# Block 1's late LayerNorms: sums placed behind the early products, and no modulation dots emitted in the product parts ahead of them

## The chip, the cores and the metric

The kernel runs on one NeuronCore of one Trainium2 chip. Five engines work side by side, each through its own list of instructions in a fixed order: TensorE (PE), VectorE (DVE), ScalarE (ACT), GpSimd (POOL) and SyncE (SP), which issues all loads. The metric is the time of one execution on the device in microseconds (us); less is better.

## The reference, cut to what matters

Two transformer blocks on 256 tokens of width 1024, in fp32. The first has two layers. In each, a vector `c` gives six modulation vectors (`silu(c) @ w_ada[l] + b_ada[l]`), and both LayerNorms sum over the width of the whole updated stream, so nothing behind a norm is complete before the last quarter of the product ahead of it.

```python
def layer_norm(x, g, b):
    mu = xf.mean(-1, keepdims=True)
    var = jnp.square(xf - mu).mean(-1, keepdims=True)
    return (xf - mu) * lax.rsqrt(var + LN_EPS) * g + b

def first_block(...):
    for l in range(DEPTH):                                   # 2 layers
        sh1, sc1, g1, sh2, sc2, g2 = split(silu(c) @ w_ada[l] + b_ada[l], 6)
        y = mixer(x * (1 + sc1) + sh1) @ w_o[l]
        x = layer_norm(ALPHA * x + (1 + g1) * y, ln_g[l, 0], ln_b[l, 0])
        y = swiglu(x * (1 + sc2) + sh2, w_ffn_in[l], w_ffn_out[l])
        x = layer_norm(ALPHA * x + (1 + g2) * y, ln_g[l, 1], ln_b[l, 1])
    return x

def swiglu_half_step(x, g, mod, j, w_up, w_down):            # second_block
    h = rms_norm(x, g) * (1 + mod[j + 1]) + mod[j]
    gt, up = split(h @ w_up, 2)
    return x + 0.5 * mod[j + 2] * ((silu(gt) * up) @ w_down)
```

The second block has two layers too. Each begins with such a half step on the stream `x` (the first block's result) and on a context stream `c` that the first block doesn't touch. Its nine modulation vectors exist once for each stream (from `c` and `c_ctx`) and come from the same matrix `w_ada_2[l]`.

## The kernel before, in words

**Products.** Activations lie with the width on the 128 partitions (8 tiles of 128 by 256 tokens). An fp32 product is three fp32r products: weights and activations are split into a high and a low part (`wh`, `wl` and `hh`, `hl`, line 149), and PE multiplies wh by hh, wl by hh, and wh by hl (line 131). So 128 output features of one stream cost 24 matmuls over a width of 1024. A weight unit is loaded to `raw` (up to 512 KB, three buffers), cast to `wh` on ACT and subtracted to `wl` on DVE (six buffers of each). A pair of units gives a PSUM bank `ps_mm` of which there are two. All loads go through SP's one queue in program order: a load whose buffer isn't free holds up those behind it.

**Modulation dots.** No matmul is used for the modulation vectors. Tile `adaw` (512 KB, two buffers) holds 128 rows of the modulation matrix, and one DVE instruction (line 456, output `junk`) multiplies it by the broadcast vector `cb` and sums along it. In block 1 a load serves one dot, in block 2 two (one for each stream). A generator `self.ada` makes load and dots in a fixed order of vectors, eight loads for each vector.

**The order.** The program is written out by a planner. Generators ("threads") for `x`, for `c`, and for the norms make the instructions piece by piece, and `main` picks the next piece by a clock of its own. `pace`, called between pieces, earns credit for dots by a rate for each phase and emits them; while `self.calm` is set it earns none. When the `x` thread needs a modulation vector that isn't complete, `until` emits all that is left of it at that place, one load and its dots after another. The `c` thread can't do that: it stays parked until the vector is there, and the planner goes on with others. `meet` merges a product of `x` and one of `c` on the same weights into a joint one (512 columns) when both have come to it.

**Late LayerNorms.** Three of block 1's four LayerNorms (layer 0's two, layer 1's first; below the first, second and third) are late. While the product ahead (attention's `w_o`, or the FFN's down product) comes out in four pairs of tiles, `emit` adds each pair to `x_res` (line 756, `add_gated`), makes the un-normalised operand with `late_tile` (lines 532 and 533), and adds squares and values up in two tiles `acc` (line 494). Only then `early` (lines 278 to 325) multiplies three pairs of units by the un-normalised operand in all six PSUM banks of `ps_mm`, `ps_s` and `ps_o`: 36 matmuls over the first six tiles, 12 over the last two, then 24 for each further unit (144 in all). `ln_finish` (from line 572), a thread of the highest priority, sums over the partitions by matmuls with `ones` (`ps_t`: four of `acc`, then four of `x_res` and four of `tr`, each of these over two tiles), reduces (line 587), goes through a chain of small DVE instructions (lines 348 to 359, 594), spreads the two columns by matmuls with `c_ident` (line 136), and updates `x_res` (line 610). With what that leaves, line 477 makes the normalised operand and `post` (lines 296 to 300) corrects and frees the early banks. `early` sets `calm` at its beginning and clears it at its end. The fourth LayerNorm, at the end of block 1, isn't late: behind it stand the RMS norm of `x` (`rms`: sums, line 634, chain, spread, and lines 650 to 653, which need the modulation vectors 1 and 0) and the first products of block 2. The `c` thread is started in layer 1's FFN and works on its own RMS norm and its first products there.

Of the kernel before, what the change touches and what calls it, by code (L numbers as in the profile page):

```python
# [67 lines left out]
class Block:  # L68
# [503 lines left out]
    def ln_finish(self, key, x, g, b, late=None):  # L572

        nc = self.nc
        st = self.p("t", (128, 2, 2, 2))
        (ax, lx), (aq, lq) = self.acc.pop((key, 0)), self.acc.pop((key, 1))
        sl = [slice(0, 128), slice(128, 256)]
# [84 lines left out]
    def ffn(self, h, wi, wo, emit, gate, last_gate=None):  # L662
# [4 lines left out]
        late = isinstance(h, Late)  # L667
        hf = None if late else self.ops(h)
        per = 12
        for i0 in range(0, FT, per):  # L670
# [26 lines left out]
            left = -(-(FT - i0 - ni) // per)  # L697
            yield ("need", gate if left or last_gate is None else last_gate)
            parts = [(i0 + k, min(6, ni - k)) for k in range(0, ni, 6)]
            for mp in range(4):  # L700
                blocks = (2 * mp, 2 * mp + 1)
                if late and mp < 2 and len(parts) == 1:

                    units = tuple(wo + (b,) + parts[0] for b in blocks)
                    yield ("w", units)
                    two = [self.p(tag, (128, 256)) for tag in ("mm", "s")]
                    for ks in ((0, -1), (-1, None)):
                        for u, ps in zip(units, two):
                            self.feat(ps, self.weight(u), 0, gf, 0, True, True, *ks)
                else:  # L710
                    ps = yield from self.feats(wo, blocks, gf, parts)
                    two = [ps[:, j, :] for j in range(2)]
                emit(left, mp, two)

    def ffn_pair(self, th, wi, wo, emit, gate):

# [420 lines left out]
    def block1(self, x, cx, ct):  # L1137
        nc = self.nc
        for l in range(2):
# [40 lines left out]
            yield ("need", ("a1", l, 3))  # L1180
            gb = self.ln_g[:, l, 0, :], self.ln_b[:, l, 0, :]
            h = self.ln_late(*gb, P(3), P(4))
            yield from self.half_out(("w_o", l), box["o"], 4, emit)
            self.spawn(self.ln_finish("b", x, *gb, h), -1)
            self.phase = ("f", l)
# [668 lines left out]
```

## Time and profile before

| | |
|---|---|
| runs, median | 2626.09 us |
| runs, lowest and highest (3) | 2618.99 and 2626.55 us |
| profiled execution, its own time | 2625.82 us |
| profiled execution, span of the trace | 2624.0 us |
| granted TensorE clock, mean of the span | 0.967 of full |
| PE, DVE, ACT, POOL busy | 95%, 66%, 40%, 8% |
| mean DMA rate | 156 GB/s |

The span is what the trace shows from first to last instruction; the profiled execution's own time is 1.8 us longer. All times below in rows are microseconds from the span's start. Busy PE time contains overlapping records, so two matmuls' distance is read from their starts.

### The profile page before, as it was taken

Reading aid. Unit: us, or ns where it says so; the run is one execution under the profiler, and the core shown is the slowest. Engines: PE = TensorE matmul, PEld = TensorE weight load, DVE = VectorE, ACT = ScalarE, POOL = GpSimd, SP = SyncE. Lnnn points to the kernel's source line nnn. Section 1 sums busy time; section 2 is a strip of 40 time slices with the busy share of each in tenths; the row PEclk is TensorE's granted clock in tenths of the full one; section 3 lists DMA queues with packets and bytes.
Section 4 is the critical chain, followed back from the end, with each engine's and each line's share of the span. In section 5 each row is a group of like instructions: output and inputs, shape, how many; then the busy total and the mean of one; then the engine's idle time right before and its main releaser. Section 6 shows DMA issues by size and latency. Waiting matters only on the chain.

```text
span 2624.0 us, 40217 instructions
## 1 busy us (share of the span) xinstructions
PE 2491.1 (95%) x15668; PEld 2239.9 (85%) x15668; DVE 1743.6 (66%) x3255; ACT 1046.2 (40%) x1817; POOL 220.9 (8%) x243
## 2 busy tenths in 40 slices
PE   5989998999998999999989999999999999999999
PEld 4879998989997888889788888888888888988999
DVE  6788887588887765576666757465754445576754
ACT  3555444545443222233566322222322223365543
POOL 2111003121000000000252000000000000041000
PEclk9989998889998999999989899999999999989999
DMA  7776885546763644534311245454354443431564
GB/s 280 248 235 210 287 283 188 180 147 194 232 189 115 192 145 133 155 113 137 106 32 49 85 154 171 118 171 127 114 167 146 128 129 105 129 96 42 174 192 133
DMA packets 127071, 408.92 MB, mean 156 GB/s; under 512 B 15585, under 2 KB 21281, under 8 KB 126753
## 3 DMA queue, kind: packets, MB, share of 16 engines
q1 hardware_dynamic: 126880, 406.35, 49.4%
q8 instruction: 123, 2.02, 0.3%
q14 instruction: 68, 0.55, 0.1%
HBM read 405.22 MB, written 1.07 MB: 155 GB/s over the span
## 4 chain that ended last, share of the span: by engine, by line
PE 75%; DVE 11%; DMA 6%; ACT 4%; issue 3%; POOL 1%; SPq 0%; ACTq 0%; DVEq 0%; POOLq 0%
PE ps_mm L131 65%; PE ps_o L131 3%; PE ps_s L131 3%; DMA raw<-in_w_ffn_in 3%; DVE wl L149 3%; PE ps_t L136 2%; PE ps_t L131 2%; DVE junk L456 2%; ACT wh L149 1%; DMA raw<-in_w_ffn_out 1%; DVE hmem L653 1%; DVE tr L650 1%; DMA adaw<-in_w_ada 1%; POOL tr L475 1%; ACT e L785 1%
## 5 line engine op out<-in xcount | busy, mean ns | idle before, releaser
L131 PE MATMUL ps_mm<-hmem,wh 128*128 128x256 f32 (+1 forms) x5760 | 1386.3, 331 | 49.8 <-ACT hmem L473 21.6
L131 PEld LDWEIGHTS ps_mm<-hmem,wh 128*128 128x128 f32 x5760 | 997.0, 195 | 159.3 <-ACT hmem L473 22.0
L131 PE MATMUL ps_mm<-hmem,wl 128*128 128x256 f32 (+2 forms) x2880 | 950.9, 330 | 2.1 <-DVE wl L149 2.0
L149 ACT CAST wh<-raw 128x1024 fp32r<-128x1024 f32 (+2 forms) x572 | 546.0, 958 | 867.8 <-PE ps_mm L131 371.7
L149 DVE TENSOR_TENSOR wl<-raw,wh 128x1024 fp32r<-128x1024 f32 (+2 forms) x556 | 625.5, 1128 | 355.6 <-ACT wh L149 353.4
L131 PEld LDWEIGHTS ps_mm<-hmem,wl 128*128 128x128 f32 x2880 | 558.9, 194 | 49.9 <-DVE wl L149 2.9
L131 PE MATMUL ps_mm<-g,wh 128*128 128x256 f32 (+1 forms) x2328 | 534.1, 323 | 3.8 <-ACT g L149 3.8
L456 DVE SCALAR_TENSOR_TENSOR junk<-adaw,cb 128x1024 fp8e4<-128x1024 f32 x343 | 423.1, 1233 | 27.8 <-DMA adaw<-in_w_ada 23.3
L131 PEld LDWEIGHTS ps_mm<-g,wh 128*128 128x128 f32 x2328 | 393.0, 191 | 37.5 <-ACT g L149 4.0
L131 PE MATMUL ps_mm<-g,wl 128*128 128x256 f32 (+1 forms) x1164 | 375.3, 322 | 2.5 <-DVE wl L149 2.5
L131 PEld LDWEIGHTS ps_mm<-g,wl 128*128 128x128 f32 x1164 | 222.9, 191 | 19.3 <-DVE wl L149 2.9
L965 POOL TENSOR_TENSOR kk<-kT,kk 64x512 fp32r<-64x512 f32 (+1 forms) x30 | 35.7, 1189 | 1359.6 <-ACT kk L964 1358.5
L735 DVE TENSOR_TENSOR tr<-tr,ps_mm 128x512 f32<-128x512 f32 x61 | 42.0, 688 | 144.9 <-PE ps_mm L131 144.9
L734 ACT ACTIVATE tr<-ps_mm 128x512 f32<-128x512 f32 x61 | 36.5, 598 | 242.6 <-PE ps_mm L131 242.6
L756 DVE SCALAR_TENSOR_TENSOR x_res<-ps_mm,ada_x,x_res 128x256 f32<-128x256 f32 x144 | 67.0, 481 | 92.0 <-PE ps_mm L131 91.5
L131 PEld LDWEIGHTS ps_o<-g,pt 128*128 128x128 f32 x808 | 109.4, 207 | 11.2 <-ACT pt L371 7.4
L131 PE MATMUL ps_o<-g,pt 128*128 128x64 f32 (+1 forms) x808 | 111.8, 287 | 4.8 <-ACT pt L371 4.5
L785 ACT ACTIVATE e<-e,small 128x256 f32<-128x256 f32 (+2 forms) x160 | 90.7, 568 | 34.9 <-DVE small L779 33.8
L131 PE MATMUL ps_mm<-wh,hmem 128*128 128x256 f32 x512 | 94.1, 282 | 0.0
L136 PE MATMUL ps_t<-c_ident,e 128*128 128x128 f32 x404 | 69.8, 297 | 12.9 <-ACT e L785 5.8
L131 PEld LDWEIGHTS ps_mm<-wh,hmem 128*128 128x128 f32 x512 | 79.5, 188 | 0.6 <-ACT g L371 0.6
L149 ACT CAST g<-tr 128x256 fp32r<-128x256 f32 (+1 forms) x137 | 68.3, 499 | 25.2 <-DVE tr L681 10.9
(227 smaller groups left out, 2034.5 us busy)
## 6 DMA issues: line engine op xcount, KB each, us to landing
adaw<-in_w_ada SPq DMA_DIRECT2D x231, 512.0 KB, 4.4
raw<-in_w_ffn_up SPq DMA_DIRECT2D x176, 512.0 KB, 3.9
raw<-in_w_ffn_in SPq DMA_DIRECT2D x88, 512.0 KB, 4.6
raw<-in_w_ffn_down SPq DMA_DIRECT2D x96, 384.0 KB, 3.1
raw<-in_w_ffn_out SPq DMA_DIRECT2D x48, 384.0 KB, 4.0
raw<-in_w_in SPq DMA_DIRECT2D x28, 512.0 KB, 3.7
raw<-in_w_in_ab SPq DMA_DIRECT2D x16, 512.0 KB, 6.6
raw<-in_w_o SPq DMA_DIRECT2D x16, 512.0 KB, 4.8
```

The costliest lines, as they stand in the source:

```text
L131: self.tc.keep_in_program_order(self.nc.tensor.matmul(out, left, right, start=start, stop=stop))
L136: self.tc.keep_in_program_order(self.nc.tensor.transpose(out, in_, self.ident))
L149: return (self.nc.scalar.copy(hi, src), (eng or self.nc.vector).tensor_tensor(out=lo, in0=src, in1=hi.bitcast(F32), op=OP.subtract))
L456: ins = self.nc.vector.scalar_tensor_tensor(out=self.junk, in0=raw, scalar=1.0, in1=v, op0=OP.mult, op1=OP.mult, accum_out=acc[:, j:j + 1] ...
L475: nc.gpsimd.tensor_scalar(out=h32[:, j, :], in0=src[:, j, :], scalar1=a[:, k0 + j:k0 + j + 1], scalar2=b[:, k0 + j:k0 + j + 1], op0=OP.mul ...
L650: nc.vector.scalar_tensor_tensor(out=t[:, j, :], in0=x[:, k + j, :], scalar=a[:, k + j:k + j + 1], in1=bc, op0=OP.mult, op1=OP.mult)
L653: nc.vector.scalar_tensor_tensor(out=hl[:, k + j, :T], in0=t[:, j, :], scalar=b[:, k + j:k + j + 1], in1=hh[:, k + j, :T].bitcast(F32), op ...
L734: nc.scalar.activation(sg, job.full[0], AF.Silu)
L735: nc.vector.tensor_tensor(out=sg, in0=sg, in1=job.full[1], op=OP.mult)
L756: self.nc.vector.scalar_tensor_tensor(out=x[:, k, :], in0=ps[j], scalar=gate[:, k:k + 1], in1=x[:, k, :], op0=OP.mult, op1=OP.add)
L785: nc.scalar.activation(e[:, at:at + w], e[:, at:at + w], AF.Exp, bias=nm, scale=-1.0, accum_out=sm)
L965: self.nc.gpsimd.tensor_tensor(out=there, in0=k, in1=here.bitcast(F32), op=OP.subtract)
```

## The change

Three edits. First, `ln_finish` with a late operand waits 2.5 units of the planner's clock before its first sums, so that other pieces are written out ahead of them. Second, `ffn` sets `calm` for the second to fourth pair of the last part of its down product, and clears it at the end. Third, block 1 sets `calm` ahead of the second half of the `w_o` product (it stays set until `early` clears it).

```diff
@@ def ln_finish(self, key, x, g, b, late=None):
         nc = self.nc
+        if late is not None:
+
+            yield self.after(2.5)
         st = self.p("t", (128, 2, 2, 2))
@@ def ffn(self, h, wi, wo, emit, gate, last_gate=None):
             for mp in range(4):
                 blocks = (2 * mp, 2 * mp + 1)
+                self.calm = left == 0 and mp > 0
                 if late and mp < 2 and len(parts) == 1:
...
                 emit(left, mp, two)
+        self.calm = False
@@ block 1, each layer
             h = self.ln_late(*gb, P(3), P(4))
+            self.calm = True
             yield from self.half_out(("w_o", l), box["o"], 4, emit)
             self.spawn(self.ln_finish("b", x, *gb, h), -1)
```

Numbers in names below are the program's running numbers and differ between the two programs; lines from 575 on stand 3 to 6 further down in the changed one.

On PE at the first late LayerNorm, the end of the `w_o` product (`ps_mm` of 256 columns), the four sums of `acc` and the first early products (258 columns). Before:

```order
L131 MATMUL ps_mm_1736<-hmem,wh_1739 128x256
L131 MATMUL ps_t_1781<-ones,acc_1642 128x1
L131 MATMUL ps_t_1781<-ones,acc_1640 128x1
L131 MATMUL ps_t_1781<-ones,acc_1642 128x1
L131 MATMUL ps_t_1781<-ones,acc_1640 128x1
```

and in the changed program, where the last early matmul over the sixth tile stands ahead of the sums and the first over the seventh tile behind them:

```order
L131 MATMUL ps_mm_1770<-hmem,wh_1783 128x258
L131 MATMUL ps_t_1823<-ones,acc_1642 128x1
L131 MATMUL ps_t_1823<-ones,acc_1640 128x1
L131 MATMUL ps_t_1823<-ones,acc_1642 128x1
L131 MATMUL ps_t_1823<-ones,acc_1640 128x1
L131 MATMUL ps_mm_1769<-hmem,wh_1777 128x258
```

The four sums moved behind the 36 early matmuls over six tiles. The sums of `x_res` and `tr`, which stood behind those 36, now stand behind all of the first pair and the next unit (72), and between them and the spread 48 matmuls stand instead of 36. It is so at all three late LayerNorms.

On PE at the end of block 1. Before: the fourth LayerNorm's sums (`ps_t<-ones`), products of `c` on `w_ffn_up` (`ps_mm<-hmem`), the LayerNorm's spread (`c_ident,small`), products of `c`, the RMS sums of `x` (the second `ones,acc`), their spread, and the first product of `x`.

```order
L131 MATMUL ps_t_8569<-ones,x_res 128x1 x4
L131 MATMUL ps_t_8569<-ones,tr_8567 128x1 x4
L131 MATMUL ps_mm_8574<-hmem,wh_8639 128x256
...
L136 MATMUL ps_t_8705<-c_ident,small_8623 128x128 x2
L136 MATMUL ps_t_8705<-c_ident,small_8635 128x128 x2
L131 MATMUL ps_mm_8674<-hmem,wh_8742 128x256
...
L131 MATMUL ps_t_8777<-ones,acc_8716 128x1
...
L136 MATMUL ps_t_8799<-c_ident,small_8787 128x128 x2
L131 MATMUL ps_mm_8834<-hmem,wh_8577 128x256
```

In the changed program, with the RMS sums of `c` (`acc_7383`) behind those of `x`:

```order
L131 MATMUL ps_t_8480<-ones,x_res 128x1 x4
L131 MATMUL ps_t_8480<-ones,tr_8478 128x1 x4
L136 MATMUL ps_t_8517<-c_ident,small_8499 128x128 x2
L136 MATMUL ps_t_8517<-c_ident,small_8511 128x128 x2
L131 MATMUL ps_t_8576<-ones,acc_8528 128x1
...
L131 MATMUL ps_t_8598<-ones,acc_7383 128x1
...
L136 MATMUL ps_t_8620<-c_ident,small_8586 128x128 x2
L131 MATMUL ps_mm_8651<-hmem,wh_8654 128x256
```

Before, the steps of `x` had 24, 48 and 24 matmuls of `c` between them, and `c`'s own RMS norm stood within the last down product. In the changed program no product stands between the last down product and the first one of `x`; behind that come 24 matmuls of `x`, the spread of `c`, 24 of `x` and 48 of `c`, and then 144 joint ones, where before 96 of `x` and 96 joint ones stood.

On DVE at the same place, the end of LayerNorm's update (now line 613), the last sums of squares (`acc`) and the chain of `x`'s RMS norm. Before (first rows), and in the changed program (rows behind the dots):

```order
L494 TENSOR_TENSOR acc_8716<-acc_8716,tr_8722 128x256
L610 TENSOR_TENSOR x_res<-x_res,ps_t_8705 128x512
L494 TENSOR_TENSOR acc_8716<-acc_8716,tr_8722 128x256
L494 TENSOR_TENSOR acc_8716<-acc_8716,tr_8730 128x256 x2
L634 TENSOR_SCALAR small_8784<-ps_t_8777 128x2
```

```order
L494 TENSOR_TENSOR acc_8528<-acc_8528,tr_8534 128x256
L456 SCALAR_TENSOR_TENSOR junk,ada_x_0_7929<-adaw_8552,cb_6931 128x1024
L494 TENSOR_TENSOR acc_8528<-acc_8528,tr_8542 128x256
L456 SCALAR_TENSOR_TENSOR junk,ada_c_0_7930<-adaw_8552,cb_6934 128x1024
L494 TENSOR_TENSOR acc_8528<-acc_8528,tr_8542 128x256
L456 SCALAR_TENSOR_TENSOR junk,ada_x_0_7929<-adaw_8556,cb_6931 128x1024
L637 TENSOR_SCALAR small_8583<-ps_t_8576 128x2
```

Dots of vector 0 of block 2 (`ada_x_0`, `ada_c_0`), which before were all done ahead of the last down product's end, stand between the steps: ten of them (five loads, `adaw_8513`, `8552`, `8556`, `8560` and `8564`) from LayerNorm's update to the first operand tile of `x`. Six more (`adaw_9027`, `9031`, `9035`, of vector 2) stand ahead of the first gated add of the first down product of block 2. In SP's queue the loads of `adaw_8556`, `8560` and `8564` stand behind seven loads of `w_ffn_up`:

```order
L121 DMA raw_8955<-in_w_ffn_up 128x1024
L121 DMA adaw_8556<-in_w_ada 128x1024
L121 DMA adaw_8560<-in_w_ada 128x1024
L121 DMA adaw_8564<-in_w_ada 128x1024
L121 DMA adaw_8572<-in_w_ada 128x1024
```

Other places: in layer 0's first LayerNorm and FFN, six loads with dots instead of ten stand ahead of the first load of `w_ffn_out`; the two dots inside the third LayerNorm's chain are gone; in the second half of the `w_o` product and the last three pairs of the down product ahead of the late norms no dot is left but two at the first norm. In the changed program one to three more splits of early weights stand ahead of the last `x_res` adds or the LayerNorm's update there. The loads of modulation weights by phase (layer 0's attention and FFN, layer 1's, block 2's two layers; the first ones of all left out) are 29, 38, 16, 17, 88 and 36 before, and 27, 33, 15, 17, 97 and 35 now.

## Rows read from the trace of the kernel before

**Rows 1.** The page, parts 1 and 4: busy time by engine; chain by engine.

```profile
PE 2491.1 (95%) x15668; PEld 2239.9 (85%) x15668; DVE 1743.6 (66%) x3255; ACT 1046.2 (40%) x1817; POOL 220.9 (8%) x243
...
PE 75%; DVE 11%; DMA 6%; ACT 4%; issue 3%; POOL 1%; SPq 0%; ACTq 0%; DVEq 0%; POOLq 0%
```

**Rows 2.** The page, parts 5 and 6: dots, splits, and loads of modulation weights.

```profile
L149 DVE TENSOR_TENSOR wl<-raw,wh 128x1024 fp32r<-128x1024 f32 (+2 forms) x556 | 625.5, 1128 | 355.6 <-ACT wh L149 353.4
...
L456 DVE SCALAR_TENSOR_TENSOR junk<-adaw,cb 128x1024 fp8e4<-128x1024 f32 x343 | 423.1, 1233 | 27.8 <-DMA adaw<-in_w_ada 23.3
...
adaw<-in_w_ada SPq DMA_DIRECT2D x231, 512.0 KB, 4.4
```

**Rows 3.** Timeline, PE, first LayerNorm: start, duration, instruction, idle before and releaser.

```profile
188.36 0.38 PE L131 MATMUL ps_t<-ones,acc 128*128 128x1 f32 x2 [1.79 <-POOL acc L494]
...
190.91 1.44 PE L131 MATMUL ps_t<-ones,acc 128*128 128x1 f32 x6 [2.17 <-DVE acc L494]
...
192.21 0.56 PE L131 MATMUL ps_mm<-hmem,wh 128*128 128x258 f32 x1
```

**Rows 4.** Timeline, PE, second LayerNorm.

```profile
404.68 0.38 PE L131 MATMUL ps_t<-ones,acc 128*128 128x1 f32 x2 [3.79 <-POOL acc L494]
...
406.77 1.44 PE L131 MATMUL ps_t<-ones,acc 128*128 128x1 f32 x6 [1.71 <-DVE acc L494]
```

**Rows 5.** Timeline, PE, third LayerNorm.

```profile
570.71 0.38 PE L131 MATMUL ps_t<-ones,acc 128*128 128x1 f32 x2 [1.72 <-POOL acc L494]
...
572.06 1.15 PE L131 MATMUL ps_t<-ones,acc 128*128 128x1 f32 x6 [0.97 <-DVE acc L494]
```

**Rows 6.** Timeline, DVE, third LayerNorm: reduce, first of two dots, end of the chain.

```profile
582.09 0.17 DVE L587 TENSOR_REDUCE small<-ps_t 128x4 f32<-128x8 f32 x1 [4.73 <-PE ps_t L131]
...
582.17 1.22 DVE L456 SCALAR_TENSOR_TENSOR junk<-adaw,cb 128x1024 fp8e4<-128x1024 f32 x1
...
586.56 0.16 DVE L594 SCALAR_TENSOR_TENSOR small<-small,small 128x2 f32<-128x2 f32 x1
```

**Rows 7.** Timeline, PE, first block-1 FFN: start of its first down product.

```profile
279.24 0.58 PE L131 MATMUL ps_mm<-g,wh 128*128 128x256 f32 x1 [3.80 <-ACT g L149]
```

**Rows 8.** Windows: start:end, length, busy us (instructions) by engine, clock, DMA share, GB/s.

```profile
280.00:290.00 10.00, 10.00 (x63) 9.99 (x63) 7.99 (x13) 2.51 (x3) 0.00 (x0) 0.72 0.88 291
...
290.00:320.00 30.00, 30.00 (x254) 30.00 (x253) 23.03 (x32) 11.95 (x14) 5.93 (x3) 1.00 0.88 297
...
872.00:938.00 66.00, 66.00 (x286) 53.52 (x285) 41.85 (x64) 16.81 (x23) 0.00 (x0) 1.00 0.55 167
```

**Rows 9.** Timeline, PE, last down product of block 1.

```profile
773.63 0.39 PE L131 MATMUL ps_mm<-g,wl 128*128 128x256 f32 x1 [1.34 <-DVE wl L149]
...
780.08 0.39 PE L131 MATMUL ps_mm<-g,wl 128*128 128x256 f32 x1 [1.15 <-DVE wl L149]
```

**Rows 10.** Timeline, PE, end of block 1 and start of block 2.

```profile
783.65 0.95 PE L131 MATMUL ps_t<-ones,acc 128*128 128x1 f32 x8
...
797.37 0.80 PE L136 MATMUL ps_t<-c_ident,small 128*128 128x128 f32 x4 [2.26 <-DVE small L359]
...
805.91 0.56 PE L131 MATMUL ps_t<-ones,acc 128*128 128x1 f32 x2 [3.55 <-DVE acc L494]
...
811.37 0.66 PE L136 MATMUL ps_t<-c_ident,small 128*128 128x128 f32 x2 [2.53 <-DVE small L359]
...
813.14 0.58 PE L131 MATMUL ps_mm<-hmem,wh 128*128 128x256 f32 x1 [1.11 <-ACT hmem L652]
...
827.76 0.39 PE L131 MATMUL ps_mm<-hmem,wl 128*128 128x512 f32 x1
```

**Rows 11.** Timeline, DVE, the same place: LayerNorm's last step, first block-2 tiles.

```profile
798.28 3.33 DVE L610 TENSOR_TENSOR x_res<-x_res,ps_t 128x512 f32<-128x512 f32 x5 [0.86 <-PE ps_t L136]
...
812.07 1.26 DVE L650 SCALAR_TENSOR_TENSOR tr<-x_res,ada_x,ps_t 128x256 f32<-128x256 f32 x3 [0.85 <-PE ps_t L136]
...
817.85 0.88 DVE L653 SCALAR_TENSOR_TENSOR hmem<-tr,ada_x,hmem 128x256 fp32r<-128x256 f32 x2 [0.19 <-ACT hmem L652]
```

## Prediction

> **What bounds the kernel now.** I read the page first, then the timelines of PE and DVE around block 1's four LayerNorms, then the windows. The page says that PE is the bound: 95% busy, with 75% of the chain that ended last [rows 1]. A dot is 1.23 us of DVE and a split 1.13, and a load of modulation weights is 4.4 us from issue to landing [rows 2]. DVE is the second engine on the chain (11%), so a dot costs where PE waits for DVE, and nothing elsewhere.
>
> At the late LayerNorms the reader is to see PE wait in front of the first sums for the last additions to `acc`: 1.79 and 2.17 us at the first [rows 3], 3.79 and 1.71 at the second [rows 4], 1.72 and 0.97 at the third [rows 5]; 12.2 us in all. Early products that need none of it stand behind. At the third, two dots lie within the chain from the reduce to its last step, which takes 4.6 us [rows 6]. In the first FFN of block 1 PE stands 3.80 us ahead of the down product [rows 7], and then at a lower clock: 63 matmuls started in 10 us at a granted 0.72, where 30 us at full clock hold 254, or 85 in ten [rows 8]; the DMA share is 0.88 in both windows. In the last down product of block 1 PE waits twice for a split, 1.34 and 1.15 us [rows 9]. Behind it comes the fourth LayerNorm and the RMS norm of `x`, one long chain over the small engines; PE's gaps there are 2.26, 3.55, 2.53 and 1.11 us [rows 10], because products of `c` fill the rest.
>
> **The change part by part.** I sum against the profiled execution's 2625.8 us, which is 0.3 us under the median.
>
> *Sums behind the early products.* The 12.2 us of idle time in front of the sums are filled with the 36 matmuls that need six tiles alone. That moves matmuls forward and doesn't shorten the chain by itself. What the chain starts from is the last pair of `x_res`, and its sums now stand behind 72 matmuls instead of 36. Of these the last 36 need the seventh and eighth tile, which come no earlier than before: 36 at 0.118 us [rows 8] are 4.3 us behind the last tile. Before, 36 matmuls from 192.21 on stood between [rows 3], at less than full clock. So the sums end at about the same time; behind them 48 matmuls (5.7 us) stand ahead of the spread, more than the bare chain takes: 4.6 us less two dots of 1.26 us with their readout are 2.1 us at the third [rows 6]. The spread therefore comes with PE's own matmuls, about when it did. One to three more splits at 1.13 us, and a dot, stand ahead of the `x_res` updates. First norm: +1. Second: 0, with its four dots gone from the product ahead against later tiles. Third: -2, for its two dots. Sum -1. The bounds are -12.2, if all the idle time comes back, and +5, if the added splits and dots (about four instructions of 1.2 us) all lie on the path.
>
> *Fewer dots ahead of the first FFN's down product.* Six loads with dots instead of ten stand there. Four loads of 512 KB are 2.1 MB, 7 us at the window's 291 to 297 GB/s [rows 8], and DMA is what this stretch is short of. I take the whole stall of 3.8 us and the slow start behind it, (85 - 63) x 0.118 = 2.6 us: -6.4. Bounds: -6.4 and 0, if the saved transfers only let the next weights wait for buffers.
>
> *No dots in the last down product of block 1.* Its two waits for splits stand behind dots on DVE: -2.5, bounds 0 and -2.5 [rows 9].
>
> *The end of block 1.* This is the big term. `calm` there delays vector 0 of block 2; `c`'s thread stays parked without it, so its products don't stand in the gaps any more, and the missing dots come out where `x` needs them, inside its chain. From the sums at 783.65 (call it 0) before: first product of `x` at 29.5, 96 of `c` and 96 of `x` done at 44.1 [rows 10], then 96 joint ones at 66.0/286 = 0.231 us [rows 8], 22.2 us: eight pairs for both streams at 66.3.
>
> Now: the sums take 3 us (four sets of 0.95 us for 8 records, the first beside the last adds), the bare chain 2.1 [rows 6], spread and hand-over 1.4, and the update starts at 6.5. Before, it and the sums of squares lasted from 798.28 to 805.91, 7.6 us [rows 10, 11]; three dots between them make it 11.3, so they end at 17.8. The RMS norm took 6.2 us from there to the first tile's instruction at 812.07 [rows 10, 11]: 24.0. Six dots lie between its steps, and the last two wait for a load that can be issued only when the dots of the load two before it are done (two buffers), at about 20.5; 4.4 us to landing [rows 2] and two dots give 27.4. So `x`'s first product starts at about 29, as before, but with nothing done meanwhile. Then `x`'s tiles (812.07 to 818.73, 6.7 us [rows 11]), two splits (2.3 us) and `c`'s tiles (6.7 us) follow each other on DVE, to 44, and the rest of `c`'s second pair to 47.3. The 144 joint matmuls are 33.3 us: 80.6. That is +14.3. Bounds: +8, if loads and dots find free time in the chain and the two streams' tiles overlap better, and +18, if each dot lies bare and PE, idle for 29 us, begins at the lower clock.
>
> *Vector 2.* Six more dots stand ahead of the first gated adds. Their last load stands in SP's queue behind a weight load whose buffer comes free only in the down product, near 86; 4.4 us and the dots give 94. The product's first two blocks fill both `ps_mm` banks by 86, so PE would stand about 8 us, and 1 more for a slow start (a third of the 2.6 above): +9. Bounds 0 (the buffer is free in time) and +11.
>
> *Block 2* takes nine more loads, 18 dots, 22 us of DVE at 66% busy [rows 1]; PE covers them, but for about +1 (bounds 0 and +3).
>
> Sum: -1 - 6.4 - 2.5 + 14.3 + 9 + 1 = +14.4, or 2640.2 us.
>
> One rule speaks against this place of the change. The Trainium skill, DMA: Bandwidth & Descriptors, Rules for kernel authors, says to issue a DMA early, compute, and wait for it late. By that rule the five loads whose dots fall into the norm should stand well ahead of it; had they been, the 14.3 and the 9 would be gone and the sum -8.9. The program here does the opposite, and the 4.4 us to landing in this trace [rows 2] is what it exposes.
>
> The bare chain has one good side: before, PE started slowly after its gaps twice. The Trainium skill, TensorE: Matmul & The Clock Gate, says that an idle array falls to the lower of two clocks and work brings it back. The trace agrees (0.72 behind a gap of 3.80 us [rows 7, 8]); by it one long gap would cost one slow start instead of two, some 2 us less, which lies within my bounds.
>
> **The rivals.**
> A. *The dear end is half hidden.* The loads lie ready, and the gate's six dots come before the banks fill. For it: DVE is 66% busy, and a load needs only 4.4 us. Against it: two buffers, and SP's fixed order. +14.3 + 1 (gate) + 1 - 9.9 = +6: 2632.
> B. *The late norms give back their idle time* (the other side). Place: PE ahead of the sums of `acc`. Price: -12.2 instead of -1, so +3 with all else as forecast, 2629, and with the gate hidden as in A -5, 2621; with the slow starts behind the three gaps gone as well (2.6 us each at most) -13, 2613. It decides once the `x_res` updates start 3 us or more earlier at all three. Against it: the last pair's adds and tiles don't move, and 48 matmuls stand ahead of the spread.
> C. *Little happens*: `c`'s products are only reordered, PE has as much to do as before, and gains and losses cancel: 2626. Against it: PE's 29 us without a product.
>
> **How the numbers follow.** The forecast, 2640, has 0.58 (its own range 2631 to 2653); A 0.18; B 0.14; C 0.10. About 0.3%, 7.9 us, is what a measurement of this kernel can tell from no change, so slower begins at 2634. Of the forecast 0.55 lies above that, of A 0.05: slower 0.60. Of B 0.10 lies under 2618, of C 0.02: faster 0.12. The rest, 0.28, is the same. The range reaches from B with the gate hidden to the upper bound of the end of block 1: 2620 to 2655.
>
> **What the profile after would show.** The forecast is right if, behind the last down product of block 1, PE has no product for 25 us or more; if dots lie between the steps of `x`'s RMS norm with a wait for `adaw`; if 144 joint matmuls end some 14 us later counted from the sums; and if PE waits for line 756's successor (now 761) in the first down product of block 2. The first FFN's stall of 3.8 us should shrink. At the late norms the early products should start right behind the product ahead, with the `x_res` updates within 2 us of where they were. It would be wrong if those updates come 3 us earlier, if the gate's dots are done before the banks fill, or if the stall in the first FFN turns up elsewhere in that FFN.

## The result, and the profile after

The changed kernel takes 2632.22 us, the median of 20 runs (2621.94 to 2641.86); the kernel before takes 2616.47 us in 20 runs of the same job (2606.40 to 2626.55). The ratio is 1.0062, with a 95% interval of 1.005 to 1.0075: 15.7 us slower. The forecast was 2640.2, 14.4 us slower than 2625.8. The size of the change is thus off by 1.3 us, and most of the 8 us between 2640 and 2632 is the starting point: the one profiled execution of before lay 9 us over the median that these 20 runs show.

The page of the changed kernel, part 1, against [rows 1]: PE has 14 us less to show as busy, in a program that is slower.

```profile
PE 2476.7 (94%) x15620; PEld 2223.8 (85%) x15620; DVE 1738.6 (66%) x3253; ACT 1046.4 (40%) x1815; POOL 221.4 (8%) x243
```

**The end of block 1.** The timeline of PE in the changed kernel, from the sums behind the last down product to the end of the first down product of block 2, against [rows 10] (start, duration, instruction, idle before and releaser):

```profile
770.25 0.95 PE L131 MATMUL ps_t<-ones,acc 128*128 128x1 f32 x8
772.32 1.22 PE L131 MATMUL ps_t<-ones,x_res 128*128 128x1 f32 x8 [1.12 <-DVE x_res L761]
...
776.95 1.09 PE L136 MATMUL ps_t<-c_ident,small 128*128 128x128 f32 x4 [2.52 <-DVE small L359]
788.57 0.56 PE L131 MATMUL ps_t<-ones,acc 128*128 128x1 f32 x2 [10.53 <-DVE acc L494]
...
798.03 0.66 PE L136 MATMUL ps_t<-c_ident,small 128*128 128x128 f32 x2 [4.20 <-DVE small L353]
800.23 0.58 PE L131 MATMUL ps_mm<-hmem,wh 128*128 128x256 f32 x1 [1.54 <-ACT hmem L655]
...
818.31 0.39 PE L131 MATMUL ps_mm<-hmem,wl 128*128 128x512 f32 x1
...
851.43 0.40 PE L131 MATMUL ps_mm<-g,wh 128*128 128x512 f32 x1
...
863.95 0.77 PE L131 MATMUL ps_mm<-g,wh 128*128 128x512 f32 x1 [6.91 <-DVE c_res L761]
...
881.84 0.40 PE L131 MATMUL ps_mm<-hmem,wh 128*128 128x512 f32 x1
```

and before, the first row behind the joint products and the first behind the down product:

```profile
849.76 0.40 PE L131 MATMUL ps_mm<-g,wh 128*128 128x512 f32 x1
...
871.53 0.40 PE L131 MATMUL ps_mm<-hmem,wh 128*128 128x512 f32 x1
```

In the changed kernel PE has no product from 770.25 to 800.23, only sums and spreads. The joint matmuls begin 48.1 us behind the first sums (47.3 forecast) and end at 81.2 (80.6 forecast; 66.1 before). At 863.95 PE then stands 6.91 us for the gated add (some 8 forecast). The product ends at 111.6; before, it ends 87.9 us behind 783.65.

The timeline of DVE in the same stretch, the first and last of ten dots, the reduce between them, and the first tile of `x`; then the first and last of vector 2's six dots and the gated add behind them:

```profile
776.92 1.22 DVE L456 SCALAR_TENSOR_TENSOR junk<-adaw,cb 128x1024 fp8e4<-128x1024 f32 x1
...
791.30 0.16 DVE L637 TENSOR_SCALAR small<-ps_t 128x2 f32<-128x2 f32 x1 [1.74 <-PE ps_t L131]
...
797.94 1.22 DVE L456 SCALAR_TENSOR_TENSOR junk<-adaw,cb 128x1024 fp8e4<-128x1024 f32 x1
...
799.16 0.48 DVE L653 SCALAR_TENSOR_TENSOR tr<-x_res,ada_x,ps_t 128x256 f32<-128x256 f32 x1
...
853.62 1.22 DVE L456 SCALAR_TENSOR_TENSOR junk<-adaw,cb 128x1024 fp8e4<-128x1024 f32 x1
...
861.12 1.22 DVE L456 SCALAR_TENSOR_TENSOR junk<-adaw,cb 128x1024 fp8e4<-128x1024 f32 x1
...
862.46 0.48 DVE L761 SCALAR_TENSOR_TENSOR x_res<-ps_mm,ada_x,x_res 128x256 f32<-128x256 f32 x1
```

The reader is to see that no dot has a wait for `adaw` at its end: the loads come in time. What the dots themselves cost, and what the missing products of `c` cost, is left to the experiments. Windows over this stretch (start:end, length, busy us and instructions by engine, clock, DMA share, GB/s), first before, then changed:

```profile
770.00:900.00 130.00, 117.98 (x640) 102.60 (x639) 97.88 (x183) 45.12 (x70) 4.23 (x4) 0.93 0.48 150
```

```profile
770.00:900.00 130.00, 101.52 (x475) 84.36 (x474) 107.64 (x220) 39.35 (x64) 0.00 (x0) 0.86 0.48 154
```

PE is busy 16.5 us less, and the granted clock falls from 0.93 to 0.86.

**The late norms.** PE in the changed kernel at the first norm (four rows), then the first normalised product of the second and of the third:

```profile
189.64 0.95 PE L131 MATMUL ps_t<-ones,acc 128*128 128x1 f32 x8
...
202.38 0.60 PE L136 MATMUL ps_t<-c_ident,small 128*128 128x128 f32 x4
...
213.58 0.55 PE L131 MATMUL ps_mm<-hmem,wh 128*128 128x256 f32 x1 [7.75 <-DVE tr L297]
...
426.84 0.55 PE L131 MATMUL ps_mm<-hmem,wh 128*128 128x256 f32 x1 [7.96 <-DVE tr L297]
...
590.06 0.55 PE L131 MATMUL ps_mm<-hmem,wh 128*128 128x256 f32 x1 [7.72 <-DVE tr L297]
```

and the same three products before:

```profile
217.73 0.55 PE L131 MATMUL ps_mm<-hmem,wh 128*128 128x256 f32 x1 [3.31 <-DVE tr L297]
...
434.12 0.55 PE L131 MATMUL ps_mm<-hmem,wh 128*128 128x256 f32 x1 [4.64 <-ACT x_res L619]
...
599.14 0.35 PE L131 MATMUL ps_mm<-hmem,wh 128*128 128x256 f32 x1 [3.23 <-DVE tr L297]
```

The sums wait for nothing any more, but for the 12.2 us that stood there [rows 3 to 5] the three waits ahead of the first normalised product, at the far end of the chain, are longer by 4.44, 3.32 and 4.49: 12.3 us. Counted from the end of the product ahead, the first update of `x_res` starts 22.2, 20.4 and 22.0 us behind it, where before it was 21.1, 21.2 and 20.1: it came 3 us earlier at none of the three.

**The first FFN.** The wait in its first down product [rows 7] is gone, and the second down product begins 93.6 us behind the first, where before it was 100.6. But a new wait stands in that second (last) down product. PE in the changed kernel:

```profile
369.15 0.58 PE L131 MATMUL ps_mm<-g,wh 128*128 128x256 f32 x1 [4.62 <-ACT g L149]
```

and DVE ahead of it, the instruction that completes layer 1's vector 0 (`ada_a`), and the last two of six dots that stand from 352.73 on:

```profile
323.62 0.16 DVE L419 SCALAR_TENSOR_TENSOR ada_a<-ada_a,c_b_ada 128x8 f32<-128x8 f32 x1
...
364.09 1.23 DVE L456 SCALAR_TENSOR_TENSOR junk<-adaw,cb 128x1024 fp8e4<-128x1024 f32 x1 [0.56 <-DMA adaw<-in_w_ada]
...
367.10 1.23 DVE L456 SCALAR_TENSOR_TENSOR junk<-adaw,cb 128x1024 fp8e4<-128x1024 f32 x1 [0.90 <-DMA adaw<-in_w_ada]
```

The operand `g` that PE waits for comes by way of a DVE instruction behind these dots, and the last four of the six wait 0.56 to 0.90 us each for their loads. The gate of this part (`last_gate`) didn't bring them there all at once: the vector that it asks for was complete at 323.62, 45 us ahead of the stall, and the six dots come one by one, 2 to 3 us apart. Behind the stall the granted clock from 370 to 380 us is 0.74, where before it is 1.00. From its first matmul to its end the second down product takes 36.6 us instead of 29.0, so the 7 us gained ahead of it are lost again.

### The profile page after: what moved, and what is told of

It is laid out like the page before. It is cut to its first block, busy times and chain, and to the rows that moved or that the text cites. A ratio compares the mean times of both kernels' runs of the same rounds, so it can differ in the third digit from the quotient of the medians.

```text
span 2623.6 us, 40156 instructions
## 1 busy us (share of the span) xinstructions
PE 2476.7 (94%) x15620; PEld 2223.8 (85%) x15620; DVE 1738.6 (66%) x3253; ACT 1046.4 (40%) x1815; POOL 221.4 (8%) x243
## 5 line engine op out<-in xcount | busy, mean ns | idle before, releaser
L131 PE MATMUL ps_mm<-hmem,wh 128*128 128x256 f32 (+2 forms) x5728 | 1376.7, 331 | 66.6 <-DVE tr L297 23.4
L131 PEld LDWEIGHTS ps_mm<-hmem,wh 128*128 128x128 f32 x5728 | 985.2, 193 | 179.4 <-issue 26.3
L131 PEld LDWEIGHTS ps_mm<-hmem,wl 128*128 128x128 f32 x2864 | 551.4, 193 | 48.1 <-DVE wl L149 0.7
L456 DVE SCALAR_TENSOR_TENSOR junk<-adaw,cb 128x1024 fp8e4<-128x1024 f32 x343 | 423.1, 1233 | 32.6 <-DMA adaw<-in_w_ada 26.7
L761 DVE SCALAR_TENSOR_TENSOR x_res<-ps_mm,ada_x,x_res 128x256 f32<-128x256 f32 x144 | 66.8, 481 | 93.8 <-PE ps_mm L131 93.6
L790 ACT ACTIVATE e<-e,small 128x256 f32<-128x256 f32 (+2 forms) x160 | 90.8, 569 | 29.8 <-DVE small L784 28.4
```

Source lines behind the costliest of these rows:

```text
L131: self.tc.keep_in_program_order(self.nc.tensor.matmul(out, left, right, start=start, stop=stop))
L456: ins = self.nc.vector.scalar_tensor_tensor(out=self.junk, in0=raw, scalar=1.0, in1=v, op0=OP.mult, op1=OP.mult, accum_out=acc[:, j:j + 1] ...
L761: self.nc.vector.scalar_tensor_tensor(out=x[:, k, :], in0=ps[j], scalar=gate[:, k:k + 1], in1=x[:, k, :], op0=OP.mult, op1=OP.add)
L790: nc.scalar.activation(e[:, at:at + w], e[:, at:at + w], AF.Exp, bias=nm, scale=-1.0, accum_out=sm)
```

## The experiments

All compare with the kernel before on the same chip. Stages below are read from the timelines of PE: a norm (N1 to N3) lasts from the end of the product ahead to the first normalised product; "end" from the last down product of block 1 to the end of the first one of block 2. A product ends with its last matmul, whose modelled end lies some 0.2 us behind the next start, so "end" is 0.2 less than the differences of starts above. "Dots" are those that stand on DVE ahead of the fourth LayerNorm's reduce. Vectors 1 and 0 of block 2 have all their dots with 128: twelve vectors of eight in block 1, and two of sixteen. The kernel reports a vector as complete only when `self.ada` is asked for the next load (the `yield` of line 432 stands ahead of line 442), and on DVE its last addition (line 439) shows about when.

| kernel | ratio (95%) | dots | N1 | N1 to N2 | N2 | N2 to N3 | N3 | N3 to end of block 1 | end |
|---|---|---|---|---|---|---|---|---|---|
| before | | 135 | 31.2 | 183.2 | 33.2 | 134.9 | 30.2 | 184.7 | 87.7 |
| before, again | | 135 | 31.3 | 181.5 | 34.1 | 138.7 | 28.5 | 183.6 | 87.4 |
| changed | 1.0062 (1.005, 1.0075) | 118 | 31.0 | 184.1 | 29.2 | 132.4 | 30.8 | 180.4 | 111.4 |
| changed, again | 1.0047 (1.003, 1.0064) | 118 | 30.4 | 181.3 | 29.3 | 139.8 | 30.8 | 181.2 | 113.5 |
| calm_not_l1 | 1.0049 (1.0032, 1.0065) | 122 | 30.4 | 182.4 | 29.2 | 135.1 | 30.8 | 180.0 | 111.1 |
| wo_only | 1.0072 (1.0047, 1.0097) | 127 | 29.5 | 188.5 | 28.8 | 138.4 | 29.2 | 179.5 | 110.0 |
| deficit_only | 1.0067 (1.0045, 1.0088) | 127 | 31.1 | 180.8 | 32.2 | 135.0 | 30.1 | 175.4 | 106.1 |
| calm_l1_only | 1.0019 (1.0003, 1.0035) | 130 | 30.9 | 185.2 | 33.5 | 144.6 | 28.6 | 179.9 | 88.3 |
| vec0_forced | 1.0054 (1.0035, 1.0073) | 132 | 30.3 | 182.1 | 29.2 | 134.8 | 30.8 | 187.4 | 98.0 |
| rate_up | 0.9999 (0.9986, 1.0012) | 133 | 31.3 | 183.4 | 29.8 | 134.9 | 30.8 | 180.1 | 88.2 |
| rate_both | 1.0036 (1.0021, 1.0052) | 147 | 32.1 | 189.4 | 32.1 | 136.1 | 30.8 | 180.4 | 91.7 |
| sums_alone | 0.9983 (0.9968, 0.9999) | 135 | 32.8 | 177.0 | 34.9 | 134.9 | 30.8 | 181.2 | 87.3 |
| sums_again | 0.998 (0.9965, 0.9995) | 135 | 32.2 | 177.1 | 34.3 | 135.4 | 31.4 | 180.9 | 87.2 |
| sums_short | 0.9997 (0.9979, 1.0015) | 135 | 28.6 | 182.8 | 35.7 | 138.7 | 26.7 | 179.9 | 87.4 |

**One part alone: the sums.** Only the first edit stays.

```diff
-                self.calm = left == 0 and mp > 0
...
-        self.calm = False
...
-            self.calm = True
```

> The first edit alone: the sums of the late norms behind the early products, all dots where they were. Theory (the idle time ahead of the sums only moves to the wait ahead of the first normalised product, and the loss comes from dots that are missing at the end of block 1): c's products still stand in the gaps at the end of block 1, time within 3 us of before, ratio 0.999 to 1.001; idle PE time of about 4 us ahead of the sums gone at each late norm, and 4 us more ahead of the first normalised product. Rival (the sums' new place costs time itself): 1.003 or more. Rival (idle time comes back in full, 12 us): 0.996 or less.

Measured 2611.85 us, 4.6 less than before, a little under the expected 0.999 to 1.001. The norms don't give it: N1 and N2 are up to 2 us longer, N3 as with all edits. Four to six us come from the first FFN behind N1, in which no wait of PE reaches 1 us, and some 3 from layer 1's FFN. It was run once more, beside the kernel with both rates raised:

> The first edit alone once more, on the same chip as the kernel with both rates raised. If its gain was real: 0.997 to 0.9995 of the kernel before. If it was scatter of the granted clock: 0.9995 to 1.002.

2611.81 us, again 4.5 less, and the same 177.1. The gain is real. In the first FFN it goes with the order of loads: in SP's queue five loads of modulation weights stand between the first norm and the first load of `w_ffn_out`, where before there are eight. With all edits there are four, in wo_only, the third edit alone, seven (stall of 2.40 us, no gain), and in sums_short below eight (2.28 us, no gain).

**Forcing vector 0 early.** All edits, and ahead of the last part of layer 1's down product:

```diff
+            if left == 0 and self.phase == ("f", 1):
+                self.until(("x", 0, 0))
```

> All three edits, and all dots of block 2's vector 0 that are still missing emitted ahead of the last part of layer 1's down product. Theory: c is no longer parked, its products stand in the gaps again, and the 24 us lost from the last down product of block 1 to the end of block 2's first down product come back, less a few us for the dots and loads forced there; what the change gains elsewhere (8 us) stays: 2606 to 2613 where before has 2616, ratio 0.996 to 0.999. Rival (the loss lies in the number of dots that block 2 takes over, wherever they stand): ratio stays at 1.004 or more.

Missed, and the time is the rival's, 1.0054. `c` is back in the gaps and the end falls to 98.0, but the part ahead of it grows by 7 us, and within the end PE waits for the sums of the fourth LayerNorm and of `x`'s RMS norm, whose inputs stand on DVE behind dots. PE in this kernel:

```profile
788.27 1.44 PE L131 MATMUL ps_t<-ones,acc 128*128 128x1 f32 x6 [5.64 <-DVE acc L494]
...
814.29 0.56 PE L131 MATMUL ps_t<-ones,acc 128*128 128x1 f32 x2 [7.37 <-DVE acc L494]
```

**Which place delays vector 0?** The prediction named the calm in layer 1's down product. All edits without it, and it alone:

```diff
-                self.calm = left == 0 and mp > 0
+                self.calm = left == 0 and mp > 0 and self.phase == ("f", 0)
```

> All three edits, but no calm in layer 1's down product (its dots are emitted at the usual rate there). Theory (the dots missing since layer 0 park c, before that product begins): the end of block 1 stays bare of c's products, PE stands about 25 us without a product, ratio 1.004 to 1.007, as with the whole change. Rival, as the prediction put it (calm in layer 1's down product delays vector 0): ratio 0.996 to 0.999, c's products back in the gaps.

```diff
+                self.calm = left == 0 and mp > 0 and self.phase == ("f", 1)
...
+        self.calm = False
```

> The kernel before with calm in layer 1's last down product alone. Theory: vector 0 is complete before that product, so c's products stay in the gaps; a few dots move into block 2: ratio 0.999 to 1.002. Rival, as the prediction put it: c parked, 20 us or more lost, ratio 1.007 or more.

The prediction's place fell, and both expectations came out. Without that calm the end is still 111.1 and the time 1.0049; with it alone the end is 88.3 and the time 1.0019. What the kernels with a long end share is the column of dots: under 128.

**The deficit by itself.** The kernel before with one number changed, which takes eight dots out of layer 1's FFN:

```diff
-RATE = {('b', 0): 0.306, ('f', 0): 0.238, ('b', 1): 0.144, ('f', 1): 0.103, ('x', 0): 0.0719, ('x', 1): 0.0562}
+RATE = {('b', 0): 0.306, ('f', 0): 0.238, ('b', 1): 0.144, ('f', 1): 0.080, ('x', 0): 0.0719, ('x', 1): 0.0562}
```

> The kernel before with one number changed: the rate of dots in layer 1's FFN is 0.080 instead of 0.103, so that 27 dots instead of 35 stand between the third and the fourth norm, as in the changed kernel; no calm, no moved sums. Theory (a deficit of dots at the end of block 1 parks c, whatever made it): PE stands some 25 us without a product there, the stage to the end of the first down product takes about 111 us instead of 88, ratio 1.004 to 1.009. Rival (the loss needs the edits themselves): 0.998 to 1.002.

1.0067 with no edit at all. PE in this kernel:

```profile
781.89 1.09 PE L136 MATMUL ps_t<-c_ident,small 128*128 128x128 f32 x4 [5.70 <-DVE small L359]
790.69 0.56 PE L131 MATMUL ps_t<-ones,acc 128*128 128x1 f32 x2 [7.72 <-DVE acc L494]
...
798.97 0.58 PE L131 MATMUL ps_mm<-hmem,wh 128*128 128x256 f32 x1 [1.11 <-ACT hmem L652]
...
860.87 0.77 PE L131 MATMUL ps_mm<-g,wh 128*128 128x512 f32 x1 [5.46 <-DVE c_res L756]
```

The same three signs as with the change: a bare chain, 144 joint matmuls behind it, and the gate's stall. (It keeps the eight loads ahead of `w_ffn_out`, and the stall of rows 7 with 2.40 us.) The changed kernel ran beside it:

> The changed kernel once more, for a second profile. The first pair of profiles differs by 0.4 us where the medians differ by 16: of the stages that the edits touch the first profile gives +15 us, and takes 5 us back ahead of the first norm and 11 in block 2 behind its first down product. Theory (these 16 are the spread of single executions, which goes with the granted clock): the stage at the end of block 1 again takes 23 to 25 us more than before, the three norms and the first FFN again 4 to 13 us less, and the other parts scatter by several us. Rival (block 2 really gets faster behind its first down product): that part again takes 1737 us, where before has 1748. Ratio 1.004 to 1.008 either way.

The end came again (113.5), the norms and the first FFN are 6 us shorter than in the first profile of before, and block 2 behind its first down product is again as short as the rival said; the last run below tells how much of that is scatter.

**The deficit filled.** All edits, and the rate of layer 1's FFN raised so that 42 dots come there instead of 27:

```diff
-RATE = {('b', 0): 0.306, ('f', 0): 0.238, ('b', 1): 0.144, ('f', 1): 0.103, ('x', 0): 0.0719, ('x', 1): 0.0562}
+RATE = {('b', 0): 0.306, ('f', 0): 0.238, ('b', 1): 0.144, ('f', 1): 0.170, ('x', 0): 0.0719, ('x', 1): 0.0562}
```

> All three edits, and the rate of dots in layer 1's FFN at 0.170 instead of 0.103: 42 dots instead of 27 between the third and the fourth norm, spread over the FFN instead of forced in one place. Theory: c's products stand in the gaps and c's tiles aren't late as in the run with the forced vector; the stage at the end of block 1 takes 88 us again, give or take 3, and the 8 us gained elsewhere stay: ratio 0.996 to 0.999. Rival (after the run with the forced vector: what the calm stretches leave out costs as much wherever it is put back): ratio 1.003 or more.

The end is back at 88.2, and the time at 0.9999, above the 0.996 to 0.999 that I expected: the gain in N2 and in layer 1's FFN stands, and the scatter of stages that the edits don't touch is as large. The first FFN still holds its late stall, 4.22 us at 376.10. So both rates were raised:

```diff
-RATE = {('b', 0): 0.306, ('f', 0): 0.238, ('b', 1): 0.144, ('f', 1): 0.103, ('x', 0): 0.0719, ('x', 1): 0.0562}
+RATE = {('b', 0): 0.306, ('f', 0): 0.29, ('b', 1): 0.144, ('f', 1): 0.170, ('x', 0): 0.0719, ('x', 1): 0.0562}
```

> All three edits, with more dots in both FFNs of block 1 (rates 0.290 and 0.170 instead of 0.238 and 0.103): 40 dots instead of 32 lie between the first and the second late norm, as before the change, and 47 instead of 27 between the third and the fourth. Theory: the first FFN's gain was taken back by the dots that the gate of its last part emitted all at once (a stall of about 4 us in its second down product, seen with the change and with the raised rate of layer 1 alone). Spread out, they leave no stall there; the part from the first to the second norm is 177 to 180 us instead of 181 to 184, the end of block 1 is as before the change (first down product of block 2 ends at 88), and the time is 0.996 to 0.999 of the kernel before. Rival: that part is short of DMA, so more loads of modulation weights in it bring the stall of 3.8 us ahead of the first down product back; the part stays at 182 to 185 us and the time at 0.999 to 1.002.

Both missed: the first FFN takes 189.4 us and the time is 1.0036, worse than either range. PE in this kernel, and the dot on DVE that the second of these rows waits for:

```profile
378.85 0.39 PE L131 MATMUL ps_mm<-g,wh 128*128 128x256 f32 x1 [1.80 <-ACT g L149]
382.07 0.80 PE L131 MATMUL ps_mm<-g,wh 128*128 128x256 f32 x2 [2.72 <-DVE g L149]
```

```profile
380.44 1.23 DVE L456 SCALAR_TENSOR_TENSOR junk<-adaw,cb 128x1024 fp8e4<-128x1024 f32 x1 [2.08 <-DMA adaw<-in_w_ada]
```

The operand `g` stands behind that dot on DVE, and the dot waits 2.08 us for its load. The Trainium skill, DMA: Bandwidth & Descriptors, Rules for kernel authors, says to issue early and wait late. This dot's wait agrees: SP issued its load no earlier than 375.44, at most 5.0 us ahead of the dot. At the end of block 1 no dot waits for its load, so the runs there say nothing for or against the rule.

The late stall belongs to the third edit: every kernel that has it stalls in that second down product, and the seven runs without it show no wait of 0.8 us or more there. It is so with the third edit alone (wo_only, below), whose first product keeps its stall too. PE in wo_only:

```profile
381.41 0.39 PE L131 MATMUL ps_mm<-g,wh 128*128 128x256 f32 x1 [2.64 <-ACT g L149]
```

How the edit brings it about is open.

**One missing dot.** With the third edit alone 127 dots stand ahead:

```diff
+            self.calm = True
             yield from self.half_out(("w_o", l), box["o"], 4, emit)
```

> The third edit alone: no dots in the second half of the w_o product. 127 dots are written out ahead of the fourth LayerNorm's reduce, and vectors 1 and 0 of block 2 are complete only with 128 (96 of block 1 and 32). Theory: c waits for all of a vector, so one missing dot is enough to keep it parked, and the bare chain at the end of block 1 costs about what 10 missing dots cost. The first down product of block 2 ends 104 to 108 us behind the last one of block 1 (88 before the change), and the time is 1.003 to 1.007 of the kernel before. Rival: the cost is that of the dots within the chain; with one instead of ten it falls to 1 or 2 us, the product ends at 89 to 92 and the time is 0.999 to 1.002.

1.0072, as dear as all edits together; the end is 110.0, a little beyond the 104 to 108 expected. DVE in this kernel, the reduce, the vector's last dot and its last addition:

```profile
790.22 0.17 DVE L587 TENSOR_REDUCE small<-ps_t 128x4 f32<-128x8 f32 x1 [2.10 <-PE ps_t L131]
...
790.37 1.22 DVE L456 SCALAR_TENSOR_TENSOR junk<-adaw,cb 128x1024 fp8e4<-128x1024 f32 x1
...
791.63 0.17 DVE L439 TENSOR_TENSOR ada_c<-ada_c,c_b_ada 128x8 f32<-128x8 f32 x1
```

So the dot that the count misses comes 0.15 us behind the reduce, and in deficit_only 0.16 us. It isn't a dot that is dear, but that the vector is reported only behind the last down product: in wo_only at 791.63, in deficit_only at 777.64, 1.4 us behind their reduces. In the kernels with `c` in the gaps it is reported 17 us or more ahead (780.47 against 797.90 in vec0_forced, 752.69 against 790.98 in calm_l1_only). How much earlier it has to be was not tried. Reported too late by a step or by ten dots is nearly the same, so most of the price is `c`'s absence from the gaps and not the dots: rate_up has as many dots behind its reduce as wo_only and deficit_only, three (785.32, 792.29 and 793.55), and ends at 88.2. In these two 5.46 us of the price lie at vector 2's gate, in the changed kernel 6.91.

**A shorter chain.** The first edit, with the sums of `x_res` and the spread asked for earlier:

```diff
-        yield self.after(self.lat("add"))
+        yield self.after(0.3 if late is not None else self.lat("add"))
...
-        yield self.after(self.lat("rsqrt"))
+        yield self.after(1.8 if late is not None else self.lat("rsqrt"))
```

> The first edit, with the other two planner waits in the late norms shortened: the sums of x_res and tr stand behind 42 early matmuls instead of 72, and the spread 30 behind them instead of 48. Theory (the place of these sums sets the start of the chain, and the idle time moved to the chain's end can be had back by starting the chain earlier): each late norm 2 to 4 us shorter than with the first edit alone, ratio 0.994 to 0.997. Rival (the chain's end waits for the split and update work on DVE and POOL, not for the sums): as with the first edit alone, 0.997 to 1.000.

N1 and N3 are 4.2 and 4.1 us shorter than with the sums alone: there the place of the sums and of the spread, which this edit moves together, sets when the norm ends. N2 isn't shorter, the first FFN is 5.8 us longer, and the time shows no gain over the sums alone (the intervals overlap).

**A second profile of before.**

> The kernel before once more, for a second profile of it. If the shorter time behind the first down product of block 2 in the profile with the change (1557 us against 1568) is scatter, this profile shows 1557 to 1566 there. If the change shortens that part, it is again 1566 to 1570.

Behind the first down product of block 2 it took 1561.3 us to the last norm, where the first profile had 1567.8 and the changed kernel 1557.0 and 1558.7. Most of that difference is scatter; whether the last 2 to 4 us are the change's stays open.

## Why the prediction was right, and where it wasn't

The second profiles of both kernels lie near the medians (2617.73 and 2633.73 us), so the account is made on them: 2631.9 - 2615.9 = +16.0 us of span.

| step | forecast | measured | from |
|---|---|---|---|
| three late norms | -1 | -3.4 | -1.0, -4.8, +2.4 |
| first FFN | -6.4 | -0.2 | 181.3 - 181.5 |
| N2 to N3 | 0 | +1.1 | 139.8 - 138.7 |
| to the end of block 1 | -2.5 | -2.4 | 181.2 - 183.6 |
| end of block 1, with vector 2's gate | +23.3 | +26.1 | 113.5 - 87.4 |
| rest of block 2 | +1 | -2.6 | 1558.7 - 1561.3 |
| ahead of the first norm | 0 | -2.5 | 182.2 - 184.8 |

The sum is nearer than its terms. The first FFN, N2 to N3 and the end came out some 10 us dearer than forecast, the norms, the rest of block 2 and the part ahead of the first norm some 8.5 cheaper; that the total is off by less than 2 us is luck.

**Right, in mechanism and size:** the end of block 1. PE is bare for 30 us (29 forecast), joint matmuls end 15 us later (81.2 against 66.1, where 80.6 against 66.3 was forecast), and the gate costs 6.9 (about 8 forecast). Three details of its working were wrong. No dot waits for `adaw` in the norm, so the rule of early loads, which was to save 14.3 and 9 us, had nothing to do with it, and the 4.4 us to landing were not exposed. "`calm` there delays vector 0" named the wrong place: calm_not_l1 and calm_l1_only show that the calm in layer 1's down product is neither needed nor enough. It is the deficit of dots from the places before it; the third edit alone makes one (wo_only). And one long gap was no better for the clock than several short ones: the granted clock of the stretch fell from 0.93 to 0.86. Of the runs here, the five with 118 to 127 dots end at 106 to 114, the others, with 130 and more, at 87 to 98. That a vector reported just behind the last down product suffices is shown twice (deficit_only and wo_only); that most of the price is `c`'s parking, and not the dots in the chain, is shown by these two beside rate_up. For the size of the ten dots the runs give a bound: 111.4 to 113.5 with ten, 106.1 to 110.0 with three, so 1 to 7 us of the 24 to 26. With vector 0 and vector 2 in time, as in rate_up, the sum was to be -8.9; it measured -0.4, with no gain left in the first FFN (183.4).

**Right by luck:** "to the end of block 1". Both waits for splits are gone, but sums_alone and sums_again keep them (1.26 and 1.17, 1.06 and 1.15 us) and are as short, 181.2 and 180.9. So the 2.4 us don't come from these waits, and what they come from is open.

**Wrong, the step that failed:** "I take the whole stall of 3.8 us and the slow start behind it ... -6.4". The stall went, and the first part of the FFN is 7 us shorter; that fewer loads ahead of `w_ffn_out` go with it is what the runs bear out (four or five: no stall of 1 us; six: 1.36; seven or eight: 2.3 to 3.8). But the second down product, to which the prediction gave nothing, took it back: another stall of 3.7 to 4.6 us with a slow start behind it. The bound of no gain was the true one. The prediction named this sign (the stall turning up elsewhere in that FFN) but no mechanism for it. The third edit is what makes the late stall, as wo_only shows; that the dots in front of `g` carry it is read from the rows. Why they come to stand so, with no more of them than before, stays open.

**Mis-sized:** the norms. The first is as forecast within 2 us. The second gained 4.8 us, not 0. Four kernels with no dot between its four pairs of adds (changed, calm_not_l1, vec0_forced, rate_up) have 29 to 30 us, those with four dots there 32 to 36; four dots are 4.9 us of DVE. But rate_both has no dot there either, and 32.1, and wo_only has three, and 28.8. So the number of dots alone doesn't set it, and what does is not shown. The third lost 2.4 us (0.6 in the first pair of profiles) instead of gaining 2: the two dots in its chain were not what set its end. The sums and the spread, behind 72 and 48 matmuls, were, as sums_short shows for N1 and N3.

**Rivals.** A gave 2632, which is where the median lies, but by chance: it is +6 from a start of 2626, and the change is +15.7 from 2616. The dear end was not hidden. B fell with the waits ahead of the first normalised products, which took back the 12.2 us. C fell with the interval.

## What to carry to other kernels

When a step is slowed or moved that feeds a later consumer piece by piece, find out when the consumer is told that all pieces are there, and compare with the time at which it is asked for: here being told just behind the last product, with all pieces at hand, cost as much as ten pieces missing. Idle time in front of a chain of small operations is not a gain until the chain starts earlier; filling it only moves the wait to the other end. And work held back from one place can come out at the next gate, all at once, as vector 2's six dots do (5 to 7 us); but before a stall is put down to a gate, look whether what the gate asks for was complete long before.

## What the runs showed of the hardware

The time of one kernel goes with the mean granted clock of the run. Of 85 runs of before that list it, the 14 at 0.966 have a median of 2620.1 us and the 11 at 0.970 one of 2614.3; a straight line through all 85 gives 1.8 us for 0.001. The medians of the clock are 0.968 in these 85 and 0.9645 in the changed kernel's 20, which is 0.0035 less. The changed kernel's window 770 to 900 has 0.86 where before has 0.93, and 0.07 x 130 us of 2624 us is 0.0035 of the mean as well. So the size fits a clock that is lost in that stretch, behind 30 us without a product, and no other cause is needed beside the idle PE. It isn't shown run by run: the first pair of profiles has this window and yet the same mean, 0.967, in both. And only runs enough to cover its scatter show a change of 0.2%.
